# First sweep of a hybrid encoder layer: one written order for chunks 4 to 15

## Chip, core and metric

The kernel runs on one core of a Trainium2 chip. The metric is the device time of one execution in microseconds; lower is better. The core has five engines with a queue each: TensorE (PE, with its weight loads PEld), VectorE (DVE), ScalarE (ACT), GpSimd (POOL) and SyncE (SP, which here only issues DMAs). Each executes its own instructions strictly in the order in which they were put, and waits at an instruction until what it needs is there.

## The reference

One layer of a bidirectional encoder over 2048 positions of width 1024 in float32. A joint input projection feeds two groups of heads; the change touches only the first, gated linear attention:

```python
h = x @ w_in
# group A: q, k (256 columns each), v (512), gate (512), two low-rank inputs of the decay (16 each)
log_af = log_sigmoid(lr_f @ wg2_f + bg_f) / 16          # per key dimension; log_ab likewise
b = cumsum(log_a)                                       # within a chunk
q_dec, k_dec = q * exp(b), k * exp(-b)
o_intra = mask(q_dec @ k_dec.T) @ v                     # within a chunk
o_inter = q_dec @ state;  state = state * exp(b_last) + k_tail.T @ v
o = rms_norm(o_fwd + o_bwd) * silu(gate)
# group B: latent attention with softmax; both groups then go through one output projection,
# and the layer ends in LayerNorm(alpha * x + mixer(x))
```

## The kernel before

The kernel has three stages: a first sweep over sixteen chunks of 128 positions (`sweep_a`), a second sweep (`sweep_c`) and the softmax attention with the output projection. The first sweep goes through the chunks backwards: step `i` handles chunk `c = 15 - i`. Texts below count by `i`. Chunks 0 to 3 run by a list written by hand (`ORDER_A`); chunks 4 to 15 are issued by `step`.

All large matmuls are float32 in three parts: a value is split into a high part, which ScalarE rounds (`hi`, a copy), and a low part, the difference (`lo`, on VectorE or GpSimd), and `mm3` adds high x high, high x low and low x high.

In one chunk TensorE computes three column groups of the projection (`products(d, g)`, 24 matmuls each): group 0 has the decay's low-rank inputs and q, group 1 has k and the first head of v, group 2 the rest of v. A fourth, `gate_products`, computes the gate of the same chunk. All four take turns in two PSUM buffers (pool `ip`), so group 1 of a chunk writes into the buffer of the gate of the chunk before, and group 2 into that of group 0. `gate_end` then runs `silu` on the gate (`gs`): three ScalarE functions (lines 1503, 1505, 1507), one multiply on VectorE (1509), and a store.

Between the matmuls stand the small steps of the attention within the chunk, as generators with names `ga_...`:

- `lr`, `lrT`: the decay's inputs are split (ScalarE, VectorE), transposed on TensorE and copied (ScalarE).
- `z`: four small matmuls, then Abs, Exp, Ln on ScalarE, a step on VectorE; then `sums`: two scans on VectorE, the chunk's sums `cl`, a subtraction (`zdone`), and two Exp on ScalarE, which give the decays `E1` and `E2`. `cw` is one more small Exp.
- `qx`, `ql` and `kx`, `kl`: VectorE transposes q (k) in blocks, four stores put it to DRAM, and two loads bring it back turned.
- `q`: VectorE multiplies the turned q by `E1` (`qd`, line 980) and stores it. `k`: the same with k and `E2` (`kd`, line 994).
- `kt`: four transposes of `kd` on TensorE and a copy on ScalarE.
- `intra`: the masked product of `qd` and `kd` (`Ap`, `At`); `av`: its product with v (`Op`), a copy on ScalarE (`oi`) and a store.
- `state`: the product of `kt` and v (`Up`), scaled on VectorE (`Us`) and stored; then the running state is stored and decayed on GpSimd (`Sm`, `Sb`).
- `ga_ld(i)`, `ga_x(i)`: the load of a chunk's x and its split; the high part (`xah`) on ScalarE, the low part (`xal`) on GpSimd.

`STEPS_A` says behind which matmul group and which `k` of it a step is traced: `(1, 4): [("kt", "prev"), ...]` puts the transposes of the chunk before behind the fifth of the eight parts of group 1. For chunks 4 to 15 this is the order in which instructions are traced, not the order in which they run: the framework's planner orders each engine's queue by its own cost model, and may put a later instruction ahead of an earlier one. `in_order(last)` takes that freedom: every instruction traced inside the block goes behind the one traced before it on the same engine. `after(ins)` only puts a block's instructions behind one given instruction. The rotary angles (`rope`) are a chain of VectorE steps, one piece per chunk, and end in chunk 12 with two sine functions on ScalarE between two loads of its function table (`rope_tables`).

The last chunks store through GpSimd's queue (`STORE_POOL`). After chunk 15 the gates of chunks 0 and 1 (`xb`, from x loaded again) and the weights of the second sweep (`wmr`, `wzr`) follow.

Of the kernel before, what the change touches and what calls it, by code (L numbers as in the profile page):

```python
# [22 lines left out]
NCH = S // P  # L23
# [34 lines left out]
av.2 av.2 gs.3 cw.3 gs.3  # L58
"""

STEPS_A = {(0, 4): [("q", "prev"), ("k", "prev")], (1, 4): [("kt", "prev"), ("lrT", "cur")],
           (1, 7): [("z", "cur"), ("cw", "cur"), ("intra", "prev")], (2, 3): [("state", "prev")],
           (3, 3): [("av", "prev")]}
STEPS_A_LAST = {**STEPS_A, (1, 6): [("z", "cur"), ("cw", "cur")], (1, 7): [("intra", "prev")]}
ENGINES = tuple(getattr(mybir.EngineType, n) for n in ("PE", "Activation", "DVE", "Pool", "SP"))
LATE_ORDER = ENGINES[1], ENGINES[3], ENGINES[4]
RND = 1.5 * 2.0 ** 23
# [292 lines left out]
class K:  # L360
# [263 lines left out]
    def sweep_a(self):  # L624
        tc, nc, ins, cp = self.tc, self.nc, self.ins, self.cp
        with ExitStack() as ctx:
            wp = ctx.enter_context(tc.tile_pool(name="wa", bufs=1, reuse_waits="tile"))
            xp, ip, tr, gp = self.xab, self.ip, self.tr, self.gp
# [19 lines left out]
            with tc.tile_pool(name="sta", bufs=1, reuse_waits="tile") as sta:  # L648
# [5 lines left out]
                for g, (_, n) in enumerate(A_GROUPS):  # L654
                    k = 0
# [32 lines left out]
            ch = self.ch = [dict(cst, c=NCH - 1 - i, i=i, lr=lrs[i % 2]) for i in range(NCH)]  # L688
            self.wa = [(wah[:, k], wal[:, k]) for k in range(NK)]
            run = lambda n, i: [0 for _ in getattr(self, "ga_" + n)(ch[i])]  # L690
            ch[0]["x"] = xcur

            def step(i, steps):

                def after(g, k):
                    for n, d in steps.get((g, k), ()):
                        run(n, i if d == "cur" else i - 1)
                for g in range(3):
                    for k in self.products(ch[i], g, after):
                        pass  # L700
                    after(g, NK - 1)
                if i and ch[i]["c"] not in LATE_GATES:
                    for k in self.gate_products(ch[i]["c"], *ch[i]["x"], ip):
                        after(3, k)
                    self.gate_end(ch[i]["c"], g1)

            self.first_lr = wdone[7][0]
            step(0, {(1, 5): [("lrT", "cur")]})
            ch[1]["x"] = self.split_x(xp, xnext, NCH - 2, "xa", "dve", 2)
            run("bst", 0)  # L710
# [4 lines left out]
            gens, last = {}, {}  # L715
            for t in ORDER_A.split():
                n, i = t.split(".")
# [3 lines left out]
                    next(gens[t], None)  # L721
            for n, g in gens.items():
                assert not list(g), n
            for i in range(4, NCH):
                c = ch[i]["c"]
                if c > 0:
                    for f in (self.ga_ld, self.ga_x):
                        for _ in f(i + 1):
                            pass
                else:  # L730
                    self.xlate = [self.split_x(xp, self.load_x(NCH - 1, "xb"), NCH - 1, "xb")]
                    self.xraw = self.load_x(NCH - 2, "xb")
                step(i, STEPS_A if c else STEPS_A_LAST)
                with self.after(ch[i]["zdone"]):
                    next(rope, None)
                if i == 12:
                    assert next(rope, None) is None
                    self.rope_tables(hpi)
            i = NCH - 1
# [1302 lines left out]
```

## Time and profile before

| | us |
|---|---|
| median of 3 runs | 1288.44 (1287.33 to 1289.19) |
| profiled execution | 1288.98 |
| its span in the trace | 1287.2 |
| mean granted TensorE clock | 0.998 |
| TensorE busy | 1262.9 |
| VectorE busy | 912.8 |
| ScalarE busy | 755.5 |
| GpSimd busy | 765.9 |

The first sweep lies between about 5 and 345 us of the span. Times in profile lines are microseconds from the span's start unless marked ns. In a time line a row has start, duration, engine, line of the kernel, operation, output<-inputs, shapes and count, and in brackets how long the engine sat idle before it and what ended that. A row of the windows has the stretch, its length, the busy time of PE, PEld, DVE, ACT and POOL with the count of instructions, the granted clock, the share of the DMA engines and GB/s. A row of the waits has the waiting instruction, what it waited for, the total in us, how often, and the longest. A row of DMA issues has the transfer, the queue, the count, the size and the median time from issue to landing. SPq is SyncE's queue. A matmul's duration reaches over the next one's start, so the step from start to start is what counts.

### The profile page before, as it was taken

Reading aid. Unit: us, or ns where it says so; the run is one execution under the profiler, and the core shown is the slowest. Engines: PE = TensorE matmul, PEld = TensorE weight load, DVE = VectorE, ACT = ScalarE, POOL = GpSimd, SP = SyncE. Lnnn points to the kernel's source line nnn. Section 1 sums busy time; section 2 is a strip of 40 time slices with the busy share of each in tenths; the row PEclk is TensorE's granted clock in tenths of the full one; section 3 lists DMA queues with packets and bytes.
Section 4 is the critical chain, followed back from the end, with each engine's and each line's share of the span. In section 5 each row is a group of like instructions: output and inputs, shape, how many; then the busy total and the mean of one; then the engine's idle time right before and its main releaser. Section 6 shows DMA issues by size and latency. Waiting matters only on the chain.

```text
span 1287.2 us, 19847 instructions
## 1 busy us (share of the span) xinstructions
PE 1262.9 (98%) x7050; PEld 1110.6 (86%) x7050; DVE 912.8 (71%) x1602; ACT 755.5 (59%) x1230; POOL 765.9 (60%) x476
## 2 busy tenths in 40 slices
PE   7999999999999999999999999999999999999997
PEld 7999999998889999999788888888888888887886
DVE  6636564644565555554788888888888889479997
ACT  7544444453565665555788888888888888511110
POOL 0133232323367666661398888889999999944441
PEclk9999999999999999999999999999999999999999
DMA  8234444444755556646301111121133110376662
GB/s 293 79 97 108 113 109 109 113 105 110 226 192 195 188 198 206 207 161 212 91 1 42 41 42 42 46 61 58 58 86 96 42 41 9 123 227 193 213 194 98
DMA packets 135746, 155.25 MB, mean 121 GB/s; under 512 B 43510, under 2 KB 86142, under 8 KB 135648
## 3 DMA queue, kind: packets, MB, share of 16 engines
q1 hardware_dynamic: 127584, 151.86, 38.5%
q0 software_dynamic: 672, 2.10, 0.4%
q8 instruction: 56, 0.92, 0.3%
q10 hardware_dynamic: 7392, 0.03, 0.3%
q14 instruction: 42, 0.34, 0.2%
HBM read 100.43 MB, written 53.51 MB: 120 GB/s over the span
## 4 chain that ended last, share of the span: by engine, by line
PE 81%; DMA 5%; DVE 4%; ACT 3%; issue 3%; POOL 2%; SPq 2%; DVEq 0%; ACTq 0%; POOLq 0%
PE pz L1216 6%; PE ipm L1287 5%; PE o L424 4%; PE o L425 4%; PE o L426 4%; PE pS L1548 4%; PE pS L1550 4%; PE pS L1551 4%; PE pS L1552 4%; PE pS L1549 4%; PE ipa L424 4%; PE ipa L426 3%; PE ipa L425 3%; PE ipg L425 2%; PE ipg L424 2%
## 5 line engine op out<-in xcount | busy, mean ns | idle before, releaser
L376 POOL TENSOR_TENSOR pl<-s,ph 128x1024 fp32r<-128x1024 f32 x128 | 306.3, 2412 | 57.4 <-ACT ph L370 53.5
L1570 DVE TENSOR_TENSOR rm<-pS,rm 128x512 f32<-128x512 f32 x210 | 144.9, 690 | 35.7 <-ACT s L1557 30.1
L1557 ACT ACTIVATE s<-pS 128x1024 f32<-128x1024 f32 x128 | 131.2, 1026 | 61.4 <-PE pS L1552 50.6
L1594 DVE TENSOR_TENSOR s<-s,mb 128x1024 f32<-128x1024 f32 x128 | 151.2, 1214 | 9.1 <-PE mb L1588 9.0
L370 ACT ACTIVATE ph<-s 128x1024 fp32r<-128x1024 f32 x128 | 135.0, 1057 | 17.0 <-PE o L426 16.4
L1598 ACT ACTIVATE s<-s 128x1024 f32<-128x1024 f32 x128 | 131.4, 1050 | 12.0 <-DVE s L1594 11.9
L424 PE MATMUL ipa<-wah,xah 128*128 128x384 f32 (+1 forms) x384 | 130.8, 341 | 6.9 <-ACT wah L370 5.4
L1051 POOL TENSOR_TENSOR Sb<-Sb,Us 64x512 f32<-64x512 f32 x15 | 21.5, 1434 | 188.0 <-ACT E L961 133.7
L425 PE MATMUL ipa<-wal,xah 128*128 128x384 f32 (+1 forms) x384 | 124.7, 325 | 0.5 <-DVE wal L376 0.5
L426 PE MATMUL ipa<-wah,xal 128*128 128x384 f32 (+1 forms) x384 | 124.4, 324 | 0.0
L1548 PE MATMUL pS<-qh,ckvT_h 128*128 128x512 f32 x256 | 102.6, 401 | 1.8 <-ACT s L1557 1.0
L424 PE MATMUL o<-ph,vh 128*128 128x512 f32 x256 | 101.0, 395 | 0.0
L426 PE MATMUL o<-ph,vl 128*128 128x512 f32 x256 | 99.8, 390 | 0.0
L1550 PE MATMUL pS<-qh,ckvT_l 128*128 128x512 f32 x256 | 99.8, 390 | 0.0
L1551 PE MATMUL pS<-rh,krs 128*128 128x512 f32 x256 | 99.8, 390 | 0.0
L1552 PE MATMUL pS<-rl,krs 128*128 128x512 f32 x256 | 99.7, 389 | 0.0
L1549 PE MATMUL pS<-ql,ckvT_h 128*128 128x512 f32 x256 | 99.7, 389 | 0.0
L425 PE MATMUL o<-pl,vh 128*128 128x512 f32 x256 | 99.7, 389 | 0.0
L1621 DVE TENSOR_TENSOR ap<-ap,s 128x512 f32<-128x512 f32 x120 | 83.1, 693 | 2.6 <-ACT s L1598 0.7
L424 PEld LDWEIGHTS ipa<-wah,xah 128*128 128x128 f32 x384 | 72.9, 190 | 12.0 <-ACT wah L370 5.4
L376 POOL TENSOR_TENSOR ol<-of,oh 128x512 fp32r<-128x512 f32 x32 | 42.8, 1339 | 64.0 <-ACT oh L370 64.0
L425 PEld LDWEIGHTS ipa<-wal,xah 128*128 128x128 f32 x384 | 73.0, 190 | 1.6 <-DVE wal L376 1.1
(308 smaller groups left out, 3577.2 us busy)
## 6 DMA issues: line engine op xcount, KB each, us to landing
xcf<-xT_dram SPq DMA_DIRECT2D x16, 512.0 KB, 5.8
xr<-x_dram SPq DMA_DIRECT2D x16, 512.0 KB, 6.2
out_dram<-rr SPq DMA_DIRECT2D x32, 256.0 KB, 2.3
xaf<-xT_dram SPq DMA_DIRECT2D x14, 512.0 KB, 4.3
oib<-oi_s SPq DMA_DIRECT2D x16, 256.0 KB, 4.3
qdb<-qd_s SPq DMA_DIRECT2D x16, 256.0 KB, 4.2
SU<-su_s SPq DMA_DIRECT2D x16, 256.0 KB, 4.0
ub<-u_s SPq DMA_DIRECT2D x16, 256.0 KB, 4.2
```

The costliest lines, as they stand in the source:

```text
L370: return nc.scalar.activation(dst, src, AF.Copy).ins
L376: return e.tensor_tensor(dst, src, hi.bitcast(F32), ALU.subtract).ins
L424: mm(out, ah, bh, start=start, stop=False)
L425: mm(out, ah, bl, start=False, stop=False)
L426: mm(out, al, bh, start=False, stop=stop)
L1548: mm(ps[:, e], kh, qh, start=True, stop=False)
L1549: mm(ps[:, e], kh, ql, start=False, stop=False)
L1550: mm(ps[:, e], kl, qh, start=False, stop=False)
L1551: mm(ps[:, e], kr, rh, start=False, stop=False)
L1552: mm(ps[:, e], kr, rl, start=False, stop=True)
L1570: V.tensor_tensor(d["rm"], src[:, e], d["rm"], ALU.max)
L1594: V.tensor_tensor(s, s, d["mb"][:, None, :].to_broadcast([P, 2, QB]), ALU.subtract)
```

## The change

Chunks 4 to 15 are traced inside `in_order`, so their instructions run on every engine in the order in which they are written. That order differs from what was traced before in these points:

- The split of the next x comes behind the gate's functions of the chunk before, since tracing order now holds.
- `q` runs in its own chunk, behind k=2 of the gate's matmuls, and no longer in the next; chunk 4 still also does chunk 3's. `k` moves from k=4 to k=3 of the next chunk's group 0.
- `z` is traced in three parts: up to its VectorE step, then `intra`, then the scans and sums, and the two Exp and `cw` only at the end of group 2.
- x is loaded two chunks ahead, at k=2 of group 1; x of chunk 5 ahead of the loop. The x for the late gate of chunk 0 is loaded at the end of chunk 14.
- The rope's steps stay outside of the written order.

```diff
-STEPS_A = {(0, 4): [("q", "prev"), ("k", "prev")], (1, 4): [("kt", "prev"), ("lrT", "cur")],
-           (1, 7): [("z", "cur"), ("cw", "cur"), ("intra", "prev")], (2, 3): [("state", "prev")],
-           (3, 3): [("av", "prev")]}
-STEPS_A_LAST = {**STEPS_A, (1, 6): [("z", "cur"), ("cw", "cur")], (1, 7): [("intra", "prev")]}
+STEPS_A = {(0, 3): [("k", "prev")], (1, 2): [("ld", "next")], (1, 4): [("kt", "prev"), ("lrT", "cur")],
+           (1, 7): [("z", "cur", 5), ("intra", "prev"), ("z", "cur", 4)], (2, 3): [("state", "prev")],
+           (2, 7): [("z", "cur"), ("cw", "cur")], (3, 2): [("q", "cur")], (3, 3): [("av", "prev")]}
+STEPS_A_FIRST = {**STEPS_A, (0, 3): [("q", "prev"), ("k", "prev")]}
+STEPS_A_LAST = {**STEPS_A, (1, 2): [], (1, 6): [("z", "cur", 5)], (1, 7): [("intra", "prev"), ("z", "cur", 4)]}
...
+            begun = {}
+
+            def some(n, i, count):
+                g = begun.setdefault((n, i), getattr(self, "ga_" + n)(ch[i]))
+                for _ in range(count):
+                    next(g)
+
             def step(i, steps):
 
                 def after(g, k):
-                    for n, d in steps.get((g, k), ()):
-                        run(n, i if d == "cur" else i - 1)
+                    for n, d, *count in steps.get((g, k), ()):
+                        j = {"prev": i - 1, "cur": i, "next": i + 2}[d]
+                        if n == "ld":
+                            if j < NCH:
+                                next(self.ga_ld(j))
+                        elif count:
+                            some(n, j, *count)
+                        elif (n, j) in begun:
+                            for _ in begun.pop((n, j)):
+                                pass
+                        else:
+                            run(n, j)
...
+            next(self.ga_ld(5))
             for i in range(4, NCH):
                 c = ch[i]["c"]
-                if c > 0:
-                    for f in (self.ga_ld, self.ga_x):
-                        for _ in f(i + 1):
+                with self.in_order(last):
+                    if c > 0:
+                        for _ in self.ga_x(i + 1):
                             pass
-                else:
-                    self.xlate = [self.split_x(xp, self.load_x(NCH - 1, "xb"), NCH - 1, "xb")]
-                    self.xraw = self.load_x(NCH - 2, "xb")
-                step(i, STEPS_A if c else STEPS_A_LAST)
+                    else:
+                        self.xlate = [self.split_x(xp, self.xb, NCH - 1, "xb")]
+                        self.xraw = self.load_x(NCH - 2, "xb")
+                    step(i, STEPS_A_FIRST if i == 4 else STEPS_A if c else STEPS_A_LAST)
+                    if c == 1:
+                        self.xb = self.load_x(NCH - 1, "xb")
```

## The prediction

> **What bounds the kernel now.** I read the page's busy shares, then the waits of TensorE's weight loads between 80 and 345 us, then the chain of waits inside one chunk of the first sweep, then stage windows by chunk, and last the time lines of that chunk engine by engine.
>
> ```profile
> PE 1262.9 (98%) x7050; PEld 1110.6 (86%) x7050; DVE 912.8 (71%) x1602; ACT 755.5 (59%) x1230; POOL 765.9 (60%) x476
> ```
> ```profile
> PEld ipa L424 <- DVE gs L1509: 4.1, 11, 0.4
> PEld kt L1002 <- DVE kd L994: 1.4, 1, 1.4
> ```
> ```profile
> 82.19:104.87 22.68, 22.68 (x149) 21.07 (x148) 13.07 (x21) 9.60 (x22) 9.12 (x6) 1.00 0.44 113
> 104.87:126.36 21.49, 21.36 (x139) 19.86 (x137) 11.97 (x21) 8.82 (x18) 6.21 (x4) 1.00 0.42 114
> ...
> 255.43:276.94 21.51, 21.38 (x138) 19.89 (x137) 12.95 (x22) 8.83 (x18) 6.47 (x4) 1.00 0.39 102
> 276.94:298.49 21.55, 21.41 (x138) 19.75 (x137) 8.98 (x18) 12.65 (x22) 6.09 (x4) 1.00 0.40 98
> 298.49:321.43 22.94, 21.61 (x138) 19.88 (x137) 10.01 (x18) 8.83 (x18) 6.63 (x6) 1.00 0.45 124
> ```
>
> TensorE sets the pace; the windows are chunks 4, 5 (the first of eight alike), 12 (the last of them), 13 and 14, at a granted clock of 1.00. A chunk takes 21.5 us and the other engines are busy 6 to 13 us of it. So the edit can win only what TensorE idles in chunks 4 to 15, and the waits name it: 11 waits for the gate's product (`gs`), 0.37 us each, and one long wait in chunk 14 for the decayed k (`kd`). The chain through chunk 10's start shows the gate wait from within:
>
> ```profile
> 212.12 0.24 PE ipg L425
> 212.48 0.92 issue
> 213.40 0.59 ACT gs L1503
> 214.01 0.64 ACT gs L1505
> 214.67 0.64 ACT gs L1507
> 215.34 0.70 DVE gs L1509
> 216.08 0.45 PE ipa L424
> ```
> ```profile
> 212.44 1.06 ACT L370 ACTIVATE xah<-xaf 128x1024 fp32r<-128x1024 f32 x1 [2.00 <-PE ipg L425]
> ...
> 215.77 0.28 ACT L370 ACTIVATE lr<-ipa 128x32 fp32r<-128x32 f32 x2 [0.46 <-PE ipa L426]
> ```
>
> The first matmul of column group 1 needs the PSUM buffer that chunk 9's gate product filled, so it waits until that gate's three functions and its multiply are over. The 0.92 us of "issue" is no hardware delay: ScalarE spent it on the next x's high part (`xah`, 1.06 us), which was put in front.
>
> **The gate ahead of x.** Here is TensorE at that place.
>
> ```profile
> 212.19 0.39 PE L426 MATMUL ipg<-wgh,xal 128*128 128x512 f32 x1
> 212.41 0.29 PE L424 MATMUL ipa<-wah,xah 128*128 128x288 f32 x1
> ...
> 215.44 0.29 PE L426 MATMUL ipa<-wah,xal 128*128 128x288 f32 x1
> 215.57 0.38 PE L1002 MATMUL kt<-ident,kd 128*128 128x128 f32 x2
> ...
> 216.37 0.34 PE L425 MATMUL ipa<-wal,xah 128*128 128x384 f32 x1
> 216.54 0.35 PE L426 MATMUL ipa<-wah,xal 128*128 128x384 f32 x1
> ...
> 218.82 0.38 PE L1002 MATMUL kt<-ident,kd 128*128 128x128 f32 x2
> ```
>
> The last gate matmul ends at 212.58. `lr` started 0.04 us after its matmul (215.44 + 0.29 to 215.77), `xah` 0.09 us after its own (212.12 + 0.24 in the chain), so with no x in front the gate starts near 212.65 instead of 213.40. From there to TensorE the chain's own rows give 216.08 - 213.40 = 2.68 us: the buffer is free at 215.33. Group 0 ends its issue at 215.57. The wait goes, with 0.24 us to spare; what is late next is TensorE itself.
>
> How much comes back: from 215.57 to the second matmul of group 1 (216.37) now pass 0.80 us; without a wait one matmul step does, 0.17. That is 0.63, but in that time two of the four transposes of kd ran as filler (218.82 to 219.04 shows 0.22 for such a pair), and the written order moves them to the other pair, behind k=4 of group 1. Net 0.41 us for each chunk whose group 1 follows a gate.
>
> **What stands behind what now.** On ScalarE `xah` moves behind the gate: it starts near 214.4 and ends at 215.5, just before `lr` can start at 215.77. Nothing waits for `xah` but VectorE's neighbour GpSimd, whose low part (`xal`) is needed a whole chunk later. On VectorE `kd` moves from before the gate's multiply to after it, at about 215.2, and `lr`'s low part and the transpose of q now queue behind it.
>
> ```profile
> 210.89 1.37 POOL L1070 TENSOR_TENSOR Sb<-Sb,cw 64x512 f32<-64x512 f32 x1
> ...
> 213.62 2.40 POOL L376 TENSOR_TENSOR xal<-xaf,xah 128x1024 fp32r<-128x1024 f32 x1 [1.36 <-ACT xah L370]
> ```
> ```profile
> 211.28 1.53 DVE L994 TENSOR_TENSOR kd<-k,E 128x512 f32<-128x512 f32 x1
> ...
> 216.09 0.19 DVE L376 TENSOR_TENSOR lr<-ipa,lr 128x32 fp32r<-128x32 f32 x1
> ...
> 255.75 0.68 DVE L994 TENSOR_TENSOR kd<-k,E 128x512 f32<-128x512 f32 x1
> ```
>
> `kd` costs 0.68 us alone and 1.53 us beside GpSimd; in that row it ends 0.55 us after GpSimd's multiply (210.89 + 1.37 = 212.26 to 212.81). In the new place `xal` comes 0.12 us behind `xah` (213.50 to 213.62), at about 215.6, so `kd` is 0.4 us ahead and takes 0.68: done at 215.9; with 1.53, at 216.8. The transposes are due at 215.57 + 15 x 0.174 = 218.2 (k=4 of group 1, 24 matmuls to the group; step from 216.37 and 216.54). So 1.4 us or more to spare, priced at nothing; if the cover went, each us beyond it would cost a us a chunk. [...]
>
> Moving q's decay is worth nothing by itself: the planner already ran it in its own chunk. So is the earlier x load: x loads sat well ahead already. On SP the load goes behind q's four stores. There q's two loads now stand ahead of all k stores, and the state's two stores ahead of k's two loads:
>
> ```profile
> 229.17 0.48 SPq L1044 DMA_DIRECT2D su_s<-Us  x1
> ```
> ```profile
> k<-kx_s SPq DMA_DIRECT2D x24, 128.0 KB, 2.6
> ...
> xbf<-xT_dram SPq DMA_DIRECT2D x2, 512.0 KB, 3.8
> ```
>
> With four issues of some 0.5 us from 229.17 the k loads are out at 231.2 and land at 233.8, 0.3 us after the next chunk starts (212.41 + 21.1); `kd` is asked for 2.8 us after that start and its transposes 5.8 us after it. Hidden. GpSimd's three state multiplies move behind k=3 of group 2, in time when it was idle. The rope's own VectorE steps stay free for the planner, after the chunk's scans as before.
>
> **The rope tables, chunk 13.** ScalarE's sine block is pinned behind chunk 12's gate.
>
> ```profile
> 279.86 1.28 ACT L618 ACT_TABLE_LOAD   x1
> ...
> 282.41 1.28 ACT L620 ACT_TABLE_LOAD   x1
> 283.70 0.29 ACT L370 ACTIVATE lr<-ipa 128x32 fp32r<-128x32 f32 x2
> ```
>
> The block takes 283.70 - 279.86 = 3.84 us. Before, `xah` was already over and the planner put the transpose of `lr` later. Written: gate over 2.1 us after the chunk's start, block to 6.0, `xah` to 7.0, `lr` and its low part to 7.6; TensorE stands at that transpose at 3.16 + 2.61 + 0.43 = 6.2. It stalls 1.4 us. Bounds: nothing (if the planner slips the block elsewhere) to 2. [...] The row has 1.28 us from a load to what follows, and I keep it.
>
> **Chunk 14** lost 22.94 - 21.52 = 1.42 us more than its neighbours because k's loads had been put last on SP:
>
> ```profile
> 297.83 1.98 SPq L811 DMA_DIRECT2D k<-kx_s  x2
> ```
> ```profile
> 302.12 0.81 DVE L994 TENSOR_TENSOR kd<-k,E 128x512 f32<-128x512 f32 x1 [6.44 <-DMA k<-kx_s]
> ```
>
> In the written order they stand ahead of q's store and the chunk is stretched by the sine stall, so by the schedule above they land 3 us before `kd` is asked for. The 1.42 us goes.
>
> **The end of the sweep.** Chunk 15's group 1 gains 0.41 too, but the weights of the next sweep load behind k's last loads on SP:
>
> ```profile
> 336.09 1.12 SPq L811 DMA_DIRECT2D k<-kx_s  x2
> 337.31 4.95 SPq L468 DMA_DIRECT2D wmr<-wB_dram  x8
> ```
>
> Those hang on the landing of k's stores, not on TensorE, so I count no gain there. The late x (`xb`) is now loaded only at chunk 14's end, lands 3.8 us later and can hold `lr` of chunk 15 by up to 0.6 us; I take 0.3, between nothing and 0.6.
>
> **The sum.** Chunk 4 to 14, eleven starts at 0.41: -4.5. Sine stall +1.4, chunk 14 -1.4, end +0.3: **-4.2 us**. The profiled execution took 1288.98 us (span 1287.2), 0.54 above the median 1288.44; so 1284.8 in its terms, **1284.2** beside the median. Bounds: without the sine stall and with chunk 15's gain -6.3 (1282.1).
>
> **Rivals.**
> A, the forecast: -2.6 to -6.3 us. For it: the same seven rows of the chain recur in every chunk.
>
> [...]
>
> C, slower: the gap loses its filler. If the gate's functions start less than 0.2 us earlier (held by something new ahead of them on ScalarE), the wait still ends last, while the two transposes no longer fill it: 12 x 0.22 = +2.6, with the sine stall +1.4 and chunk 14 -1.4 that is 1291.0. The same if the order does not take effect at this place. Against it: nothing but the drained first product (`oi`) stands ahead of the gate.
>
> D, slower: k's loads, now behind the state's stores and behind q's landing, become the wait of every chunk as in chunk 14. It decides if they land 4 us later than worked out. Eleven times 1.42 is +15.6, against -4.2: 1299.8. Against it: 4 us of margin in a queue that idles.
>
> **How the numbers follow.** A 0.64, B 0.20, C 0.09, D 0.07. About 0.2% (2.6 us) is what a measurement of this kernel can tell from no change. So faster 0.64, same 0.20, slower 0.16. The range goes from the bound of A, 1282.1, up over B to 1289.6, which leaves out C and D and little of A; A's own range is 1282.1 to 1285.8.
>
> **What would show it.** Right: chunks 5 to 12 at 21.1 us; the wait of the weight loads for `gs` gone; `gs` directly after the gate's matmuls on ScalarE with `xah` behind it; four transposes of `kd` together; chunk 13 near 22.5, chunk 14 near 21.1. Wrong: a wait of `kt` for `kd`, or of `lrT` for `lr`, in every chunk (B); 0.5 us still between group 0 and group 1 (C); `kd` idle before a DMA of k (D); or a sweep that is 4 us shorter with the weights of the next sweep no earlier.

## The result, and the profile after

The changed kernel takes 1285.43 us, the median of 10 runs (1284.27 to 1286.10), against 1289.01 us for the kernel before (10 runs, 1287.33 to 1289.92). The ratio is 0.9973 with a 95% interval of 0.9964 to 0.9981: faster by 3.6 us, between 2.4 and 4.6. The forecast was 1284.2, in a range of 1282.1 to 1289.6. The profiled execution took 1286.1 us, its span is 1284.3, its mean granted clock 0.998, as before.

First the busy shares from the page and the waits of TensorE's weight loads between 80 and 345 us (the waiting instruction, what it waited for, total, times, longest). In the new file the lines behind the edit are 21 higher and those of the helpers one, so `gs`' multiply is now L1530, `kd` L1015, `kt` L1023.

```profile
PE 1259.7 (98%) x7050; PEld 1109.9 (86%) x7050; DVE 899.4 (70%) x1602; ACT 755.5 (59%) x1230; POOL 761.1 (59%) x476
```
```profile
PEld kt L1023 <- DVE kd L1015: 2.1, 1, 2.1
PEld lrT L933 <- DVE lr L377: 1.4, 1, 1.4
PEld Op L1047 <- DVE At L1040: 1.0, 1, 1.0
```

The 11 waits for `gs` are gone, and so is the wait in chunk 14. Two new single waits stand in their place, of `lrT` in chunk 13 and of `kt` behind the sweep. The third row is not new: before, the same wait came at 347.00, just outside of this stretch. Here are the chunks after: chunk 4, chunk 5, then 12, 13 and 14, and as the last row the end of the sweep, from chunk 15's first matmul to the first matmul of the second sweep (`ipm`).

```profile
82.21:104.27 22.06, 22.06 (x148) 20.80 (x147) 10.93 (x20) 9.86 (x21) 6.29 (x4) 1.00 0.43 116
104.27:125.39 21.12, 21.12 (x138) 19.86 (x137) 11.06 (x20) 8.84 (x18) 5.92 (x4) 1.00 0.43 113
...
252.08:273.19 21.11, 21.11 (x138) 19.85 (x137) 10.65 (x20) 8.84 (x18) 5.92 (x4) 1.00 0.46 121
273.19:295.64 22.45, 21.32 (x138) 19.82 (x137) 9.68 (x18) 12.63 (x22) 5.73 (x4) 1.00 0.39 107
295.64:316.76 21.12, 21.12 (x138) 19.85 (x137) 9.26 (x17) 8.83 (x18) 6.59 (x5) 1.00 0.33 90
316.76:355.05 38.29, 36.08 (x222) 31.69 (x221) 20.14 (x32) 22.05 (x42) 13.02 (x15) 1.00 0.79 267
```

In a row of 21.11 or 21.12 us TensorE's busy time equals the length: such a chunk has no idle time left. The same last stretch before was this:

```profile
321.43:358.23 36.80, 36.09 (x222) 31.76 (x221) 18.76 (x31) 21.62 (x42) 11.58 (x13) 1.00 0.75 244
```

So the account by stages, chunk 4 to the end of the sweep, from the two profiles:

| stage | before | after | difference | forecast |
|---|---|---|---|---|
| chunk 4 | 22.68 | 22.06 | -0.62 | -0.41 |
| chunks 5 to 12 | 172.07 | 168.92 | -3.15 | -3.28 |
| chunk 13 | 21.55 | 22.45 | +0.90 | +0.99 |
| chunk 14 | 22.94 | 21.12 | -1.82 | -1.83 |
| end of the sweep | 36.80 | 38.29 | +1.49 | +0.3 |
| sum | | | -3.20 | -4.2 |

What follows the sweep differs by a few tenths between single profiles. One steady chunk in the time line (chunk 10, it starts at 209.86) shows the new order from within:

```profile
210.06 0.60 ACT L1524 ACTIVATE gs<-ipg 128x512 f32<-128x512 f32 x1 [2.17 <-DMA qd_s<-qd]
...
211.89 1.04 ACT L371 ACTIVATE xah<-xaf 128x1024 fp32r<-128x1024 f32 x1
212.02 0.69 DVE L1530 TENSOR_TENSOR gs<-ipg,gs 128x512 f32<-128x512 f32 x1 [3.86 <-ACT gs L1528]
212.63 0.68 DVE L1015 TENSOR_TENSOR kd<-k,E 128x512 f32<-128x512 f32 x1
213.02 0.33 PE L425 MATMUL ipa<-wah,xah 128*128 128x384 f32 x1
213.06 2.51 POOL L377 TENSOR_TENSOR xal<-xaf,xah 128x1024 fp32r<-128x1024 f32 x1 [6.06 <-ACT xah L371]
```

The gate's functions come first, `xah` behind them, and the buffer is free at 212.71, 0.31 us before group 1 (the 128x384 row) asks for it. `kd` starts 0.43 us ahead of `xal`, takes 0.68 us, and the busy time of VectorE falls by 13 us.

### The profile page after: what moved, and what is told of

The parts are those of the page before. It is cut to its first block, busy times and chain, and to the rows that moved or that the text cites. A ratio compares the mean times of both kernels' runs of the same rounds, so it can differ in the third digit from the quotient of the medians.

```text
span 1284.3 us, 19837 instructions
## 1 busy us (share of the span) xinstructions
PE 1259.7 (98%) x7050; PEld 1109.9 (86%) x7050; DVE 899.4 (70%) x1602; ACT 755.5 (59%) x1230; POOL 761.1 (59%) x476
## 4 chain that ended last, share of the span: by engine, by line
PE 82%; DMA 5%; DVE 4%; ACT 2%; issue 2%; POOL 2%; SPq 2%; DVEq 0%; POOLq 0%; ACTq 0%
PE pz L1237 6%; PE ipm L1308 5%; PE o L425 4%; PE o L426 4%; PE o L427 4%; PE pS L1569 4%; PE pS L1570 4%; PE pS L1572 4%; PE pS L1571 4%; PE pS L1573 4%; PE ipa L425 4%; PE ipa L427 4%; PE ipa L426 4%; PE ipg L427 2%; PE ipg L425 2%
## 5 line engine op out<-in xcount | busy, mean ns | idle before, releaser
L377 POOL TENSOR_TENSOR xal<-xaf,xah 128x1024 fp32r<-128x1024 f32 x12 | 29.7, 2477 | 87.8 <-ACT xah L371 87.8
```

What stands on the lines that cost most here:

```text
L377: return e.tensor_tensor(dst, src, hi.bitcast(F32), ALU.subtract).ins
```

## The experiments

Beside the kernels with x first, the gate alone, the tables moved and the late x earlier, the kernel before took 1288.65 us (25 runs); beside the later ones 1288.77 us (15 runs: chunk 15 rearranged, the three edits together, kd last, q in the next chunk) and 1289.05 us (9 runs: SP in order, k held ahead of q). The theory: the gain is the place of the gate's functions (the PSUM buffer is free in time); the written order is what keeps `kd`, k's loads and `xal` in an order that hides them, and it has its own price at two places. Rivals: the gain comes from the order as a whole, whatever stands first; or `kd` beside GpSimd takes the gain back.

**x ahead of the gate, in the written order.** Everything as changed, but the split of the next x is traced in front of the gate's functions.

```diff
                     for k in self.gate_products(ch[i]["c"], *ch[i]["x"], ip):
                         after(3, k)
+                    if 4 <= i < NCH - 2:
+                        run_x(i + 2)
                     self.gate_end(ch[i]["c"], g1)
...
-                        for _ in self.ga_x(i + 1):
-                            pass
+                        if i == 4:
+                            run_x(i + 1)
```

> The changed kernel with one move: for chunks 5 to 14 the split of the next x is written ahead of the gate's functions again; all else keeps the written order. Gate theory: the gate's multiply again ends at 3.6 us into the chunk, group 1 waits 0.5 us for its buffer, and no transposes of kd fill that time; chunks 5 to 12 take 21.7 us instead of 21.1, slower than the changed kernel by about 10 x 0.62 = 6.2 us, so some 2.6 us slower than before. Order theory (the gain comes from the written order of the other engines, SP above all): chunks stay near 21.1 us and the time stays near 1285.4.

Measured: 1290.57 us (11 runs), ratio 1.0016 (1.0007 to 1.0026); that is 1.9 us slower than before, where 2.6 was expected. Its waits and its chunk 10:

```profile
PEld ipa L425 <- DVE gs L1533: 5.8, 10, 0.6
```
```profile
212.87:234.58 21.71, 21.36 (x138) 19.87 (x137) 10.21 (x19) 8.82 (x18) 6.20 (x4) 1.00 0.40 107
```

The gate waits are back, and the chunk is 0.2 us longer than before the change: two of `kd`'s transposes no longer fill the gap. That is the price that rival C was given. In a steady chunk the order by itself gains nothing; the gate's place in it does. What the order alone does give is chunk 14: 21.71 us in this kernel, 22.94 before.

**The gate's place alone.** The kernel before, with the split of x held behind the gate's third function. All else is left to the planner.

```diff
-        nc.scalar.activation(t, t, AF.Exp, scale=-1.0)
+        self.gs3 = nc.scalar.activation(t, t, AF.Exp, scale=-1.0).ins
...
-                    for f in (self.ga_ld, self.ga_x):
-                        for _ in f(i + 1):
+                    for _ in self.ga_ld(i + 1):
+                        pass
+                    with self.after(self.gs3):
+                        for _ in self.ga_x(i + 1):
                             pass
                 else:
-                    self.xlate = [self.split_x(xp, self.load_x(NCH - 1, "xb"), NCH - 1, "xb")]
+                    with self.after(self.gs3):
+                        self.xlate = [self.split_x(xp, self.load_x(NCH - 1, "xb"), NCH - 1, "xb")]
```

> The kernel before with one edit: ScalarE's split of the next x is queued behind the last function of the gate before it; the planner still orders all the rest. Gate theory: chunks 5 to 12 take 21.1 us as in the changed kernel, and the wait of the weight loads for gs is gone; what the planner does with the sine block and with k's loads in chunk 14 is open, so 1284.5 to 1286.5 in all. Order theory: chunks stay at 21.5 us and the time at 1289.

Measured: 1287.6 us (11 runs), ratio 0.9991 (0.9982 to 1.0000): the total misses the 1284.5 to 1286.5 that were expected, and its interval just reaches no change. Chunks 12, 13 and 14, then VectorE in chunk 14 and SP ahead of it:

```profile
251.92:273.03 21.11, 21.11 (x138) 19.85 (x137) 12.43 (x22) 8.83 (x18) 6.47 (x4) 1.00 0.39 104
273.03:294.64 21.61, 21.36 (x138) 19.78 (x137) 8.97 (x18) 12.64 (x22) 6.08 (x4) 1.00 0.31 75
294.64:321.00 26.36, 22.93 (x138) 21.43 (x137) 10.20 (x17) 8.83 (x18) 6.58 (x6) 0.94 0.45 126
```
```profile
298.75 1.99 DVE L997 TENSOR_TENSOR kd<-k,E 128x512 f32<-128x512 f32 x1 [6.95 <-DMA k<-kx_s]
300.66 0.68 DVE L1512 TENSOR_TENSOR gs<-ipg,gs 128x512 f32<-128x512 f32 x1
```
```profile
292.74 0.47 SPq L1070 DMA_DIRECT2D su_s<-Sm  x1
293.30 0.53 SPq L490 DMA_DIRECT2D xbf<-xT_dram  x1
293.94 2.08 SPq L814 DMA_DIRECT2D k<-kx_s  x2
```

Chunks 5 to 12 reach the same 21.11 us without any written order. Chunk 14 loses 5.2 us: the planner had put k's loads on SP behind the next chunk's store of the state and the late x, `kd` waited for them, and the gate's multiply stood behind `kd` in VectorE's queue: the gate's third function ended at 296.77, the multiply ran at 300.66. The long wait of before in chunk 14 (for `kd`) has become a wait for the gate that stands behind it: TensorE idles 3.42 us, and its clock is lower after that (0.55 from 301.40 to 305.00, 0.94 over the chunk).

**The same, and SP in order in chunks 13 and 14.** One line more on the last kernel:

```diff
-                step(i, STEPS_A if c else STEPS_A_LAST)
+                with self.in_order(last if i in (13, 14) else {}, ENGINES[4:] if i in (13, 14) else (None,)): step(i, STEPS_A if c else STEPS_A_LAST)
```

> The kernel before with the next x's split pinned behind the gate's third function, and with one thing more: in chunks 13 and 14 SP alone keeps the order in which its instructions are written, so that k's loads stand ahead of chunk 14's store of the state and of the load of the late x. Everything else is left to the planner. If the gate's place and k's loads are the whole gain, and the written order on the other engines is only a means: chunks 5 to 12 at 21.11 us, chunk 13 at 21.6 us, chunk 14 at 21.1 us instead of 26.35, chunk 15 starts near 315.8 us, the end of the sweep is as before (36.4 to 36.8 us), and the time is 1282.0 to 1283.0 us, 2.5 to 3 us under the changed kernel, which pays for its order with the sine stall and the late kd. If the written order itself is worth something: not under 1285 us.

Measured: 1282.41 us (5 runs, 1282.23 to 1282.93); ratio 0.9947 (0.9934 to 0.9961). Chunks 13, 14 and the end of the sweep:

```profile
273.27:294.84 21.57, 21.32 (x138) 19.73 (x137) 8.98 (x18) 12.64 (x22) 5.26 (x4) 1.00 0.42 114
294.84:315.96 21.12, 21.12 (x138) 19.85 (x137) 9.18 (x17) 8.83 (x18) 6.23 (x6) 1.00 0.44 119
315.96:352.39 36.43, 35.85 (x222) 31.77 (x221) 19.48 (x31) 22.44 (x44) 12.21 (x14) 1.00 0.75 249
```

All three came as expected, and the time with them. k's loads leave at 291.38, 3.46 us ahead of chunk 14's start; in the last kernel it was 0.70 us. Its interval does not touch that of the changed kernel: with the gate first and k's loads in place, the written order on the other engines costs about 3 us. The rows already show where most of it lies: chunk 13 is 0.88 us shorter than in the changed kernel, the end of the sweep 1.86 us.

**The sine tables in the gap.** As changed, but the two table loads and the two functions come behind chunk 13's z, where ScalarE idles.

```diff
+STEPS_A_TABLES = {**STEPS_A, (1, 7): STEPS_A[1, 7] + [("tables", "cur")]}
...
-                    self.rope_tables(hpi)
```

> The changed kernel with the rope's sine block moved from between the gate and x of chunk 13 to behind chunk 13's mask copy on ScalarE, where ScalarE sat idle 3.7 us. Theory: the stall of TensorE at the transpose of lr goes, chunk 13 takes 21.1 instead of 22.45 us, 1.3 us faster than the changed kernel, about 1284.1. Rival (the stall only moves: a later chunk or the sweep's end waits instead): no change, 1285.4.

Measured: 1284.01 us (5 runs), ratio 0.9965 (0.9953 to 0.9978). Chunk 13 after this edit, and ScalarE in chunk 13 of the changed kernel:

```profile
273.55:294.67 21.12, 21.12 (x138) 19.86 (x137) 9.93 (x18) 12.64 (x22) 5.86 (x4) 1.00 0.40 108
```
```profile
275.35 1.28 ACT L619 ACT_TABLE_LOAD   x1
...
277.91 1.28 ACT L621 ACT_TABLE_LOAD   x1
279.20 1.06 ACT L371 ACTIVATE xah<-xaf 128x1024 fp32r<-128x1024 f32 x1
280.17 0.27 ACT L371 ACTIVATE lr<-ipa 128x32 fp32r<-128x32 f32 x2
```

In the written order `xah` and `lr` stand behind the 3.85 us block (275.35 to 279.20), and the transpose of `lr` waits. The stall is 22.45 - 21.11 = 1.34 us and it goes, as was expected. In the rows each load lasts 1.28 us, and the next instruction starts 1.29 us after the load's start.

**The late x earlier.** The x for the late gate (`xb`) is loaded at k=2 of chunk 14's group 1 instead of at its end.

```diff
                             if j < NCH:
                                 next(self.ga_ld(j))
+                            else:
+                                self.xb = self.load_x(NCH - 1, "xb")
...
-                    if c == 1:
-                        self.xb = self.load_x(NCH - 1, "xb")
```

> The changed kernel with the x of the late gate loaded at k=2 of chunk 14's group 1, where earlier chunks load theirs, and no longer at the end of chunk 14. Late-load theory: the split of that x starts right behind the gate, lr of chunk 15 is 1.9 us earlier, the wait of kd's transposes after the sweep (1.8 us) shrinks or goes, and the time falls by 1 to 1.5 us to about 1284.2. Rival (GpSimd's stores and state multiplies hold kd at the end of the sweep, not the load): the transposes still wait 1 us or more, no change.

Measured: 1285.48 us (9 runs), ratio 0.9976 (0.9967 to 0.9986): no change, so the theory of the late load fell in the form it had. The load came sooner and `lr` of chunk 15 with it (from 321.98 to 320.02), but the wait of `kt` for `kd` after the sweep stayed. These are the rows of that wait in the changed kernel:

```profile
332.21 1.12 SPq L832 DMA_DIRECT2D k<-kx_s  x2
334.91 1.39 DVE L1001 SCALAR_TENSOR_TENSOR qd<-q,E 128x512 f32<-128x512 f32 x1 [1.10 <-ACT E L984]
336.22 2.04 DVE L1015 TENSOR_TENSOR kd<-k,E 128x512 f32<-128x512 f32 x1
336.65 1.05 POOL L1091 TENSOR_TENSOR Sb<-Sb,cw 64x512 f32<-64x512 f32 x1
338.32 0.66 PE L1023 MATMUL kt<-ident,kd 128*128 128x128 f32 x4 [1.64 <-DVE kd L1015]
```

`kd` is late for several reasons at once: k's loads leave late, `qd` stands ahead of it and waits for the last Exp, and beside GpSimd it takes 2.04 us and ends 0.56 us after GpSimd's multiply (336.65 + 1.05). z's step (`za`) is not among the reasons. Here are it and the transpose of k in the changed kernel (chunk 15 starts at 316.76), then `za` in this one (start 316.67), then both before (start 321.43):

```profile
326.71 0.69 DVE L955 SCALAR_TENSOR_TENSOR za<-z,za 128x512 f32<-128x512 f32 x1 [3.80 <-ACT za L953]
327.32 0.44 DVE L824 STREAM_TRANSPOSE kx<-ipa 128x256 f32<-128x256 f32 x1
```
```profile
326.61 0.69 DVE L955 SCALAR_TENSOR_TENSOR za<-z,za 128x512 f32<-128x512 f32 x1 [5.64 <-ACT za L953]
```
```profile
330.38 0.45 DVE L803 STREAM_TRANSPOSE kx<-ipa 128x256 f32<-128x256 f32 x1 [4.72 <-DMA qx_s<-qx]
331.78 0.69 DVE L934 SCALAR_TENSOR_TENSOR za<-z,za 128x512 f32<-128x512 f32 x1 [0.95 <-ACT za L932]
```

Counted from the chunk's start, `za` comes at 9.95 us, at 9.94 with the late x earlier, and at 10.35 before. But `kx`, which the planner had put ahead of it (8.95 us), now stands behind it (10.56 us).

**Chunk 15 rearranged.** On VectorE the transpose of k ahead of z's step, the scans ahead of the mask copy; behind the sweep k is traced ahead of q.

```diff
-STEPS_A_LAST = {**STEPS_A, (1, 2): [], (1, 6): [("z", "cur", 5)], (1, 7): [("intra", "prev"), ("z", "cur", 4)]}
+STEPS_A_LAST = {**STEPS_A, (1, 2): [], (1, 6): [("z", "cur", 4)], (1, 7): [("z", "cur", 3), ("intra", "prev"), ("z", "cur", 2)]}
...
-            run("q", i)
             run("k", i)
+            run("q", i)
```

> The changed kernel with chunk 15 alone rearranged: on VectorE the transpose of k comes ahead of z's step, the two scans ahead of the mask copy, and behind the sweep k's decay comes ahead of q's. Theory for the lost end of the sweep: kd was late because of its place on VectorE, behind the scans and behind qd, beside GpSimd's state steps. Then k's loads go out near 330 us, kd runs near 333 us, right after the first of the two last Exp and before GpSimd starts on the state, the transposes of kd find it ready and TensorE's 1.64 us wait goes: 1283.6 to 1284.1 us. Rival (k's loads or the decay itself still come last): the wait stays at 1 us or more and the time at 1285.4 us. Second rival: it goes, but the weights of the second sweep come last, and the second sweep begins no earlier: also 1285.4 us.

Measured: 1284.82 us (5 runs), ratio 0.9964 (0.9951 to 0.9976). The interval holds the time of the changed kernel, so by itself it can't be told from no gain, and the 1283.6 to 1284.1 that were expected are missed. In its profile the end of the sweep takes 37.64 us and the wait of `kt` is 0.69 us. The rows show why the gain is so little; it is the rival that was named:

```profile
332.65 1.76 SPq L832 DMA_DIRECT2D k<-kx_s  x2
336.65 0.69 DVE L1015 TENSOR_TENSOR kd<-k,E 128x512 f32<-128x512 f32 x1 [1.47 <-DMA k<-kx_s]
```

`kd` takes 0.69 us here instead of 2.04, but now it is k's loads that come last, and they are late because of the late x at the head of the chunk. The planner, free again behind the sweep, also put `qd` back ahead of `kd`.

**The three edits together**: the tables in the gap, the late x earlier and chunk 15 rearranged, each as in its diff above.

> The changed kernel with three edits together: the sine tables in the gap behind chunk 13's z (worth 1.4 us by itself), the late x loaded earlier (worth nothing by itself), and chunk 15 rearranged with k ahead of q. If the gains add up: 1282.2 to 1282.8 us, 6 us under the kernel before. If the late x matters once kd no longer comes last, up to 0.5 us less. If the end of the sweep is bound by something else, 1284.0 us as with the tables alone.

Measured: 1282.81 us (5 runs), ratio 0.9951 (0.9939 to 0.9964). The end of the sweep is 37.13 us long and `kt` still waits 0.50 us. The time lies at the upper end of what was expected if the gains add up.

**k held ahead of q**, on top of the three:

```diff
-            run("k", i)
-            run("q", i)
+            with self.in_order(last):
+                run("k", i); run("q", i)
```

> The three edits together, with k's decay held ahead of q's behind the sweep, which the planner had turned round again: kd stood 1.37 us behind qd and then beside GpSimd's multiply, 2.04 us in all, and TensorE waited 0.50 us. If kd alone is late there: kd runs near 333 us and ends by 334.5 us, before GpSimd's second multiply, the wait of its transposes goes, and the time is 0.4 to 0.6 us under that kernel, 1282.2 to 1282.5 us. If k's loads land only near 334 us: half of the wait stays. If what follows (the weights of the second sweep) sets the end: no change, 1282.8 us.

Measured: 1282.02 us (5 runs, 1281.27 to 1282.79), ratio 0.9944 (0.9931 to 0.9956), where 1282.2 to 1282.5 was expected; the intervals of this kernel and the last overlap. VectorE in this one:

```profile
332.87 0.87 DVE L1017 TENSOR_TENSOR kd<-k,E 128x512 f32<-128x512 f32 x1 [1.62 <-DMA k<-kx_s]
333.66 2.04 DVE L1003 SCALAR_TENSOR_TENSOR qd<-q,E 128x512 f32<-128x512 f32 x1
```

Now it is `qd`, for which TensorE does not wait in this run, that takes 2.04 us. The wait of `kt` is gone and the end of the sweep takes 36.43 us (315.35 to 351.78), the length that the planner reaches with the gate first and SP in order. The written order without its two flaws, and the planner with its one flaw mended, take about the same time: 7.0 and 6.6 us under the kernel before.

**kd behind lr and qx.** k's decay moves from k=3 to k=7 of group 0, so that `xal` starts ahead of `kd`.

```diff
-STEPS_A = {(0, 3): [("k", "prev")], ...
+STEPS_A = {(0, 7): [("k", "prev")], ...
...
-STEPS_A_FIRST = {**STEPS_A, (0, 3): [("q", "prev"), ("k", "prev")]}
+STEPS_A_FIRST = {**STEPS_A, (0, 3): [("q", "prev")]}
```

> [...]

Two outcomes were put down. If `kd` ends about 0.55 us after `xal`, as it ended 0.55 us after GpSimd's multiply in the kernel before, TensorE waits 0.3 to 0.5 us for it in each chunk and the time is 1289 to 1291 us; if it only runs somewhat slower, chunks stay at 21.11 us and the time at 1285.4. Both are estimates of the author.

Measured: 1297.33 us (5 runs), ratio 1.0062 (1.0048 to 1.0076). GpSimd and VectorE in chunk 10 (it starts at 213.47), then chunks 12 and 13 and the end of the sweep:

```profile
216.69 2.39 POOL L377 TENSOR_TENSOR xal<-xaf,xah 128x1024 fp32r<-128x1024 f32 x1 [6.04 <-ACT xah L371]
217.70 1.93 DVE L1015 TENSOR_TENSOR kd<-k,E 128x512 f32<-128x512 f32 x1
```
```profile
256.62:278.19 21.57, 21.31 (x138) 19.76 (x137) 11.90 (x20) 8.84 (x18) 6.14 (x4) 1.00 0.43 121
278.19:305.20 27.01, 22.82 (x138) 21.27 (x137) 11.27 (x18) 12.64 (x22) 6.02 (x4) 0.94 0.33 88
...
326.79:369.17 42.38, 37.81 (x223) 33.15 (x222) 22.24 (x31) 21.92 (x42) 12.97 (x15) 0.96 0.74 242
```

`kd` ends 0.55 us after `xal` (219.08 to 219.63) and a chunk takes 21.57 us: 0.46 us more than with `kd` ahead of `xal`, inside the 0.3 to 0.5 of the first outcome. The total was missed by 6 us, though. Behind `lr`, `kd` also inherits what holds up `lr`: the sine block in chunk 13 (4.6 us more than in the changed kernel) and the late x in chunk 15 (4.1 us more). About 1.7 us of each, by the estimate in the last section, is TensorE's clock, which was 0.57 to 0.58 after the wait.

**q in the next chunk.** q's decay goes back to k=3 of the next chunk's group 0, ahead of k.

```diff
-STEPS_A = {(0, 3): [("k", "prev")], ... (3, 2): [("q", "cur")], ...
+STEPS_A = {(0, 3): [("q", "prev"), ("k", "prev")], ...
```

> The changed kernel with q's decay put back into the next chunk, behind k=3 of its group 0 and ahead of k, still in the written order. The prediction says that moving q's decay is worth nothing. If so: 21.11 us chunks and 1285.4 us. [...]

Measured: 1290.77 us (11 runs), ratio 1.0013 (1.0004 to 1.0022), just under the 1291 to 1295 us that the author estimated for the case that `xal` starts ahead of `kd` here too and `kd` ends 0.55 us after it. Chunk 10:

```profile
215.28 0.68 DVE L1001 SCALAR_TENSOR_TENSOR qd<-q,E 128x512 f32<-128x512 f32 x1
215.72 2.51 POOL L377 TENSOR_TENSOR xal<-xaf,xah 128x1024 fp32r<-128x1024 f32 x1 [6.05 <-ACT xah L371]
215.88 2.90 DVE L1015 TENSOR_TENSOR kd<-k,E 128x512 f32<-128x512 f32 x1
```

The 0.68 us of `qd` is enough for `xal` (215.72) to start ahead of `kd` (215.88). `kd` then takes 2.90 us, again ends 0.55 us after GpSimd (218.23 to 218.78), and a chunk takes 21.69 us, 0.58 more than in the changed kernel and 0.18 more than before. Chunk 13 takes 22.45 us as in the changed kernel, its sine stall covers it.

## Why the prediction was right, and where not

- **The gate wait.** Right in mechanism and size. Eight chunks alike gained 0.39 us each where 0.41 was worked out; the buffer is free 0.31 us ahead of need, forecast 0.24. The two kernels with x first and with the gate alone show that it is this place and nothing else of the order.
- **Chunk 4** gained 0.62, not 0.41. The kernel with the gate alone has the same 22.06 us there, so this too is the gate's place and not the written order. The trace of before shows what was worse than in other chunks: the gate's third function ended at 85.74, but its multiply started at 86.15, behind chunk 3's `qd` and `kd` on VectorE (from 84.94); in the changed kernel it stands ahead of both, at 85.08.
- **kd and xal.** Right: 0.68 us, 0.43 us ahead of `xal`. The danger B, a wait of `kt` for `kd` in every chunk, which takes the range up to 1289.6, was an estimate of the author's that no run of the changed kernel shows; where `kd` started behind `xal` it came, with a chunk 0.46 us longer. The margin is thin: 0.43 us, less than the 0.68 of that one VectorE instruction.
- **"Moving q's decay is worth nothing by itself."** Wrong as a statement on this order. It is so beside the planner, which ran q in its own chunk already; but in a written order q has to be put there by hand, or 0.58 us a chunk is lost and the change with it. The step that failed was the reading of a part as free because the kernel before had the same result by another way.
- **Sine stall.** Forecast 1.4, measured 1.34, taken away by moving the block.
- **Chunk 14.** Forecast -1.83 with its gate, measured -1.82. Rival D's danger was real where the order was not written: with the gate first and the planner's SP, k's loads cost 5.2 us in chunk 14.
- **The end of the sweep** is the mis-sized term: +0.3 forecast, +1.49 measured. The prediction priced the late x alone, which was to hold `lr` by 0.6 us at most, and counted no gain for chunk 15's gate. `lr` came 1.96 us later instead (321.98 against 320.02 with the late x earlier), and no matmul waited for it. The gate's gain does come: where `kd` is in time, the end of the sweep takes 36.43 us, 0.37 less than before. What the prediction left out is `kd` of chunk 15, which ends 21.5 us into the chunk (before 19.2) and costs 38.29 - 36.43 = 1.86 us. In VectorE's queue `kx` stands behind z's step, the first scan behind the mask copy (12.46 us into the chunk, before 11.08), and `qd` ahead of `kd`; on SP the late x, through `lr`, `qx` and q's stores, holds k's loads. No single edit took the wait away. By the profiles the late x alone gave nothing (38.27 us), chunk 15 rearranged 0.65 (37.64), the late x on top of that 0.51 (37.13), k ahead of q another 0.70 (36.43). The term makes up the difference between the -4.2 of the sum and the -3.2 of the two profiles (-3.6 between the medians), less what chunk 4 gave beyond its share.
- **Rivals C and D** did not come. C's price was met by the kernel with x first: 0.20 us in chunk 10, forecast 0.22. That its total (+1.9 us, forecast +2.6) is near too is in part luck: chunk 4 was 0.62 us shorter and the end of the sweep 1.45 us longer than before, which C's sum does not have.

## What to carry to other kernels

Look for the buffer that the fullest engine waits for, and put what frees it ahead of all that is merely early; check then, on each queue, what now stands behind and beside it. A written order pays for one right place with every place it fixes: pinning one function and one queue over two chunks gave about 3 us more than ordering all five engines. When several delays end within a microsecond of each other, removing one shows little or nothing (here the late x gave 0.02 us alone and 0.51 on top of another edit); the profile of that run names the next.

## What the runs showed of the hardware

The granted clock of TensorE was lower after the three stalls of 2.64, 3.42 and 4.19 us shown here. After the 4.19 us that TensorE idles for `kd` in chunk 13 of the kernel with `kd` behind `lr` (to 288.34), and after 2.64 us in its chunk 15 (to 335.38), these windows follow:

```profile
288.00:292.00 4.00, 3.66 (x14) 3.66 (x15) 0.28 (x1) 0.77 (x2) 2.22 (x2) 0.57 0.58 146
```
```profile
336.00:340.00 4.00, 4.00 (x21) 3.76 (x21) 0.00 (x0) 1.84 (x4) 0.00 (x0) 0.58 0.71 184
```

In the kernel with the gate alone it was 0.55 from 301.40 to 305.00, after 3.42 us. In the changed kernel chunk 13, with 1.13 us of idle time, and the end of the sweep, with the 1.64 us for `kd`, both have 1.00. An estimate from these rows: 4 us at 0.57 to 0.58 of the clock cost 4 x 0.42 to 0.43, about 1.7 us on top of the idle time, so a stall of 3 us in this kernel costs nearly 5.

Of VectorE beside GpSimd the traces show one constant. In each pair shown here in which `kd` took longer than its 0.68 us, it ended 0.55 to 0.56 us after GpSimd's instruction: 1.53 us long before the change, 2.04 in the changed kernel's chunk 15, 1.93 and 2.90 in chunk 10 of the kernels with `kd` behind `lr` and with q in the next chunk. What in the hardware holds it until then is not shown.
